# Turning the gated output of the linear attention: TensorE transposes, or 32x32 blocks on VectorE with a way through device memory

## The chip, the cores and the metric

The kernel runs on one core of one Trainium2 chip. The metric is the device time of one execution in microseconds. The inputs and weights are float32; every large product is made from float32r parts (a rounded high part and the difference to it).

## What is computed

Two layers over 256 positions of width 2048. Each layer projects its input once, runs three groups of heads beside each other, multiplies each group's output with a SiLU gate, and projects the concatenation back:

```python
h = x @ w_in
a_q, a_k, a_v, a_z, b_q, b_k, b_v, b_z, b_lr, m_q, m_z = jnp.split(h, cuts, axis=-1)
y_a = chunk_band_attention(heads_a(a_q), heads_a(a_k), heads_a(a_v), rel_table)      # 8 heads of 128
o_b = gla_chunk_recurrence(heads_k(b_q), heads_k(b_k), b_v, heads_k(log_g))          # 4 heads, values of 128
o_b = o_b * lax.rsqrt(jnp.mean(jnp.square(o_b), axis=-1, keepdims=True) + RMS_EPS) * gla_norm_g
y_m = memory_attention(heads_m(m_q), heads_m(mk), heads_m(mv))                       # 4 heads of 128
y = jnp.concatenate([y_a * silu(a_z), y_b * silu(b_z), y_m * silu(m_z)], axis=-1)
x = layer_norm(DEEPNORM_ALPHA * x + y @ w_out, ln_g, ln_b)
```

The change concerns `y_b * silu(b_z)`, the gated output of the linear attention: four heads of 128 columns, a quarter of the 2048 rows of the output projection.

## The kernel before

Weights stream through SBUF in pieces of 128x1024 values (`piece`, L129). For each, SP's queue loads `raw`, ScalarE rounds it to `wh` (L117), VectorE takes the difference `wl` (L118), and TensorE multiplies with both. Each of the three tiles has four buffers. A projection group of 512 columns is made of eight pieces. `ws_half` (L241) makes half a group with the weights stationary, so that its result has the columns on the partitions; `as_group` (L273) makes a whole group with the activations stationary, so that its result has the positions on the partitions.

After each piece both call `tick` (L52). It lets at most one waiting generator run up to its next `yield`, whose value is the number of ticks until it is due again. At most three generators are active once the linear attention is done, the next in `waiting` start when a place comes free. What a generator emits stands in TensorE's and SP's queues exactly there, since these two are written out in program order; the instructions of VectorE, ScalarE and GpSimd are ordered by a scheduler.

The order of a layer's groups from the place of the change on is: `G_BZ` (the gate of the linear attention, L855), then the gates of the two halves of the chunked attention and of the memory attention (`G_AZ0`, `G_AZ1`, `G_MZ`, two `ws_half` each, L862), then the output projection in four groups (L882 on). The heads of the memory attention (`m_head`, L546) run beside the gates: scores, softmax, a turn of the probabilities by `turned`, seven ticks' wait, casts to two parts, two ticks' wait, products with the values.

`turned` (L505) turns a tile in 32x32 blocks: VectorE transposes the blocks in place (L508), GpSimd's queue writes them to device memory as `home` (L510) and fetches them back in four transfers, one for each group of 32 partitions (L512). Both attentions use it for their probabilities.

`gla_gate` (L482) multiplies the linear attention's output `yraw[0]` (tile `yr0`) with the SiLU of `G_BZ`, positions on the partitions. The output projection wants columns on the partitions, so `gla_turned` (L491), a generator put at the head of `waiting`, turns it: for each half `par` of the heads, four TensorE transposes of 128x128 into one PSUM bank (L498), then one ScalarE instruction for the high part, scaled by the norm's gain (L501), and one on VectorE for the low part (L502). The result is `yq[0]`, the first quarter that the output projection reads.

`gb` (L886) are the rows of the layer norm's gain and offset for the next layer. In the first layer they reuse the buffers of `yraw`, the first those of `yr0`, and are loaded by GpSimd's queue (L888, L889). Tiles `gq` and `gk` hold the linear attention's queries and keys, and are free after it.

Of the kernel before, what the change touches and what calls it, by code (L numbers as in the profile page):

```python
# [8 lines left out]
F32 = mybir.dt.float32  # L9
# [3 lines left out]
AF = mybir.ActivationFunctionType  # L13
ALU = mybir.AluOpType
# [4 lines left out]
P = 128  # L19
D = 2048  # L20
T = 256
# [15 lines left out]
def hybrid_trunk_kernel(  # L37
# [7 lines left out]
    pe, dve, act, pool, sp = nc.tensor, nc.vector, nc.scalar, nc.gpsimd, nc.sync  # L45
# [27 lines left out]
    def enter(name, bufs=1, **kw):  # L73
        return ctx.enter_context(tc.tile_pool(name=name, bufs=bufs, **kw))
# [5 lines left out]
    hd = enter("hd", 1)  # L80
# [9 lines left out]
    def nm(s):  # L90
        uid[0] += 1
        return f"{s}_{uid[0]}"
# [4 lines left out]
    def bank():  # L97
        return psa.tile([P, 512], F32, name=nm("bk"), tag="bk")

    def scratch(shape, dtype=F32):  # L100
        return sc.tile(shape, dtype, name=nm("sc"), tag="sc")
# [4 lines left out]
    ident = cst.tile([P, P], F32, name="ident")  # L106
# [3 lines left out]
    def operand():  # L110

        x = opp.tile([P, 4, 2, T], F32R, name=nm("x"), tag="x")
        return x[:, :, 0], x[:, :, 1], x.rearrange("p j h t -> p j (h t)")
# [376 lines left out]

    def gla_turned(yraw, ng, y):  # L491

        for par in range(2):
            on = yraw[:, 2 * par:2 * par + 2].rearrange("p t (b d) -> p t b d", d=P)
            pt = bank()
            for t in range(2):
                for b in range(2):
                    pe.transpose(pt[:, b * T + t * P:b * T + (t + 1) * P], on[:, t, b], ident)  # L498
            ptv = pt.rearrange("p (b t) -> p b t", b=2)
            hi, lo = (x.rearrange("p (b r) t -> p r b t", r=2)[:, par] for x in y[:2])  # L500
            act.activation(hi, ptv, AF.Copy, scale=ng[:, 0:1])  # L501
            dve.scalar_tensor_tensor(lo, ptv, ng[:, 0:1], hi.bitcast(F32), op0=ALU.mult, op1=ALU.subtract)  # L502
            yield 1

    def turned(dst, src, n):  # L505

        blocks = scratch([P, 4, n])
        dve.transpose(blocks.rearrange("p b (g j) -> p g b j", j=32), src.rearrange("p (g b j) -> p g b j", b=4, j=32))  # L508
        home = drm.tile([P, 4, n], F32, name=nm("home"), tag=f"home{n}")
        pool.dma_start(home, blocks)  # L510
        for b in range(4):
            pool.dma_start(dst[b * 32:(b + 1) * 32], home[:, b].rearrange("(a i) n -> i a n", a=4))  # L512
# [107 lines left out]
    def columns(n):  # L620
        return slice(n * 512, (n + 1) * 512)

    def wo_pieces(l, n):

        if n < 3:
            return [w512[l, G_WO + n, pc] for pc in range(8)]
        return [[w256[l, i, pc // 2][:, pc % 2 * 512:pc % 2 * 512 + 512] for i in range(2)] for pc in range(8)]
# [141 lines left out]
    for l in range(L):  # L769
# [20 lines left out]
        gq = hd.tile([P, 2, T], F32, name=nm("gq"), tag="gq")  # L790
        gk = hd.tile([P, 2, T], F32, name=nm("gk"), tag="gk")
# [17 lines left out]
        def heads(g):  # L809
            t = hd.tile([P, 4, T], F32, name=nm("qk"), tag="qk", bufs=4)  # L810
            for i, a, b in ws_group(w512[l, g], xq):
                total(t[:, i:i + 2], a, b)
            return t
# [22 lines left out]
        yraw = [per.tile([P, 4, T], F32, name=nm("yr"), tag=f"yr{i}") for i in range(4)]  # L836
# [3 lines left out]
        for half in range(2):  # L840
            values(2 + half)
            q = heads(G_AQ0 if half == 0 else G_AQ1)
            k = heads(G_AK0 if half == 0 else G_AK1)
# [14 lines left out]
        gla_gate(acc, yraw[0])  # L858
        yq = [operand()]
        gens[0] = [gla_turned(yraw[0], gp[2], yq[0])]  # L860
        waiting[:0] = gens[0]
        for i, g in ((1, G_AZ0), (2, G_AZ1), (3, G_MZ)):  # L862
            y = operand()
# [18 lines left out]
        for n in range(WO_N):  # L882
            if last:
                g, b = scratch([P, 512]), scratch([P, 512])
            else:
                both = per.tile([P, 2, 512], F32, name=nm("gb"), tag=f"yr{n}")  # L886
                g, b = both[:, 0], both[:, 1]
# [3 lines left out]
            src = wo_pieces(l, n)  # L891
# [30 lines left out]
            if last:  # L922
                r = res[:, 1, columns(n)]
# [90 lines left out]
```

## Time and profile before

| | |
|---|---|
| median of 3 runs | 916.83 us (916.73 to 916.91) |
| the profiled execution | 916.47 us |
| its span, first to last instruction | 914.7 us |
| TensorE busy, matmuls | 907.3 us, 5420 |
| VectorE, ScalarE, GpSimd busy | 601.3, 492.2, 87.8 us |
| mean granted TensorE clock | 0.997 |

A line of a group or of the timeline names the engine, the line of the kernel, the operation, the tile written and the tiles read, then the shape and the count. In a group line the busy time in us and the mean duration of one in ns follow, and behind the next bar the idle time before them with what ended it. In a timeline line the start comes first, then the duration, with idle time before it in brackets. PE is TensorE, DVE VectorE, ACT ScalarE, POOL GpSimd, SP the queue of weight loads; `acc` are the projections' PSUM tiles and `bk` the single banks of all else. A line of the waits has the total, the count and the longest wait in us. A line of a window has TensorE's matmuls, its weight loads, VectorE, ScalarE and GpSimd in that order, then the clock, the DMA engines' busy share and GB/s. A line of transfers has the count, the size of one and the median us from issue to landing.

### The profile page before, as it was taken

The numbers are of one execution on the slowest core, as the hardware profiler recorded it, in microseconds if no ns is written. First come the engines' busy times: TensorE is split into PE (matmuls) and PEld (weight loads), VectorE is DVE, ScalarE is ACT, GpSimd is POOL, SyncE is SP. The second block draws the span as 40 slices with busy tenths as digits, with TensorE's granted clock in tenths as the row PEclk, the third lists the DMA queues.
The fourth block names the chain that finished last, engine by engine and source line by source line (L and its number), as shares of the span: only waits on it lengthen the run. The fifth ranks groups of instructions, "written<-read, shape, count | busy, mean of one in ns | idle before, by whom it ended". The sixth has DMA issues, their size and how long they took to land.

```text
span 914.7 us, 14341 instructions
## 1 busy us (share of the span) xinstructions
PE 907.3 (99%) x5420; PEld 797.9 (87%) x5420; DVE 601.3 (66%) x845; ACT 492.2 (54%) x706; POOL 87.8 (10%) x169
## 2 busy tenths in 40 slices
PE   9999999999999999999999999999999999999997
PEld 7889998998888888888888899889888888888885
DVE  6764478656576667555587666885756576766566
ACT  6654475474454666433466445754744455864340
POOL 1000000013031221000000000001121230320000
PEclk9999999999999999999999999999999999999998
DMA  9865865558575778666674466546575766686652
GB/s 302 313 222 168 298 222 165 163 194 251 186 223 182 219 208 251 209 197 193 227 255 166 145 203 202 196 148 212 184 243 190 218 196 198 203 272 202 199 162 92
DMA packets 75989, 189.33 MB, mean 207 GB/s; under 512 B 9224, under 2 KB 33160, under 8 KB 75664
## 3 DMA queue, kind: packets, MB, share of 16 engines
q1 hardware_dynamic: 69120, 173.30, 58.5%
q0 software_dynamic: 6656, 14.86, 5.9%
q8 instruction: 42, 0.69, 0.3%
q10 hardware_dynamic: 144, 0.26, 0.1%
q14 instruction: 27, 0.22, 0.1%
HBM read 181.01 MB, written 7.34 MB: 206 GB/s over the span
## 4 chain that ended last, share of the span: by engine, by line
PE 98%; DMA 1%; SPq 0%; DVE 0%; ACT 0%; issue 0%
PE acc L95 90%; PE bk L95 7%; DMA raw<-w 1%; PE bk L599 0%; PE bk L498 0%; SPq L165 0%; SPq L178 0%; PE bk L397 0%; SPq L180 0%; ACT res L755 0%; ACT wh L117 0%; DVE stats L740 0%; PE bk L344 0%; DVE res L739 0%; DVE res L691 0%
## 5 line engine op out<-in xcount | busy, mean ns | idle before, releaser
L118 DVE TENSOR_TENSOR wl<-raw,wh 128x1024 fp32r<-128x1024 f32 (+3 forms) x321 | 369.5, 1153 | 230.3 <-ACT wh L117 227.4
L117 ACT CAST wh<-raw 128x1024 fp32r<-128x1024 f32 (+3 forms) x321 | 318.9, 995 | 327.9 <-PE acc L95 237.1
L95 PE MATMUL acc<-x,wh 128*128 128x512 f32 x1248 | 396.5, 399 | 0.0
L95 PE MATMUL acc<-wh,x 128*128 128x512 f32 (+2 forms) x1236 | 356.6, 370 | 0.6 <-ACT wh L117 0.6
L95 PEld LDWEIGHTS acc<-x,wl 128*128 128x128 f32 x1248 | 234.4, 188 | 55.2
L95 PEld LDWEIGHTS acc<-wh,x 128*128 128x128 f32 x1236 | 227.2, 188 | 28.4 <-ACT wh L117 1.1
L95 PE MATMUL acc<-x,wl 128*128 128x256 f32 x1248 | 245.7, 278 | 0.0
L95 PE MATMUL acc<-wl,x 128*128 128x512 f32 (+2 forms) x618 | 228.0, 369 | 0.0
L95 PEld LDWEIGHTS acc<-x,wh 128*128 128x128 f32 x1248 | 192.2, 189 | 1.9 <-ACT wh L117 0.2
L95 PEld LDWEIGHTS acc<-wl,x 128*128 128x128 f32 x618 | 116.1, 188 | 14.6 <-DVE wl L118 0.6
L512 POOL DMA_DIRECT2D pT<-home x96 | 52.4, 553 | 56.7 <-DMA home<-sc 24.3
L510 POOL DMA_DIRECT2D home<-sc x24 | 13.4, 560 | 358.4 <-DVE sc L508 352.9
L531 ACT ACTIVATE sc<-sc,mx 128x128 f32<-128x128 f32 (+1 forms) x32 | 14.4, 449 | 18.0 <-DVE mx L529 18.0
L524 DVE SCALAR_TENSOR_TENSOR sc<-bk,bias 128x384 f32<-128x384 f32 x16 | 8.7, 542 | 11.7 <-PE bk L95 11.7
L386 ACT ACTIVATE sc<-sc 128x512 f32<-128x512 f32 x12 | 7.6, 633 | 14.7 <-DVE sc L384 14.6
L508 DVE STREAM_TRANSPOSE sc<-sc 128x384 f32<-128x384 f32 (+1 forms) x24 | 14.9, 619 | 0.6
L118 DVE TENSOR_TENSOR x<-sc,x 128x512 fp32r<-128x512 f32 x20 | 13.5, 685 | 0.7 <-ACT x L117 0.7
L118 DVE TENSOR_TENSOR x<-res,x 128x512 fp32r<-128x512 f32 (+2 forms) x14 | 10.5, 764 | 5.2 <-ACT x L117 5.2
L304 POOL DMA_DIRECT2D gwraw<-gate_w x6 | 3.1, 522 | 106.0 <-PE bk L587 105.1
L95 PE MATMUL bk<-qk,qk 128*128 128x128 f32 (+1 forms) x64 | 13.1, 327 | 0.0
L632 DVE SCALAR_TENSOR_TENSOR res<-res,acc 128x512 f32<-128x512 f32 x15 | 9.7, 684 | 5.1 <-PE acc L95 5.1
L95 PE MATMUL bk<-pT,asv 128*128 128x256 f32 (+1 forms) x64 | 13.0, 326 | 0.0
(207 smaller groups left out, 573.1 us busy)
## 6 DMA issues: line engine op xcount, KB each, us to landing
raw<-w SPq DMA_DIRECT2D x214, 512.0 KB, 4.3
raw<-w SPq DMA_DIRECT2D x64, 388.0 KB, 3.5
raw<-w SPq DMA_DIRECT2D x83, 256.0 KB, 3.6
bias<-relw SPq DMA_DIRECT2D x16, 192.0 KB, 4.3
home<-sc POOLq DMA_DIRECT2D x16, 192.0 KB, 2.7
pT<-home POOLq DMA_DIRECT2D x64, 48.0 KB, 4.0
res<-xT SPq DMA_DIRECT2D x4, 512.0 KB, 5.2
res<-xn SPq DMA_DIRECT2D x1, 2048.0 KB, 8.6
```

The source lines that it names most:

```text
L95: pe.matmul(o, l, r, start=start, stop=stop, skip_group_check=True)
L117: act.copy(hi, src)
L118: dve.tensor_tensor(lo, src, hi.bitcast(F32), op=ALU.subtract)
L304: pool.dma_start(raw[i * 16:i * 16 + 16], gate_w[l])
L386: act.activation(dd, dd, AF.Abs)
L508: dve.transpose(blocks.rearrange("p b (g j) -> p g b j", j=32), src.rearrange("p (g b j) -> p g b j", b=4, j=32))
L510: pool.dma_start(home, blocks)
L512: pool.dma_start(dst[b * 32:(b + 1) * 32], home[:, b].rearrange("(a i) n -> i a n", a=4))
L524: dve.scalar_tensor_tensor(s, pb[:, :384], SCALE, bias[h], op0=ALU.mult, op1=ALU.add)
L531: act.activation(s[:, own[t]], s[:, own[t]], AF.Exp, bias=mx[:, t:t + 1], accum_out=zs[:, t:t + 1])
L632: dve.scalar_tensor_tensor(r, r, ALPHA, acc, op0=ALU.mult, op1=ALU.add)
```

## The change

`gla_turned` uses `turned` instead of TensorE. For each half the gated output (positions on the partitions, two tiles of 2x128 columns) is turned into a tile `yT`, in the buffers of `gq` and `gk`, and the generator asks to wait six ticks after each. Then the high and low parts are taken from `yT` in SBUF, a tile of 128x128 at a time, 8 instructions on ScalarE and 8 on VectorE, because the blocks lie in another order there. The PSUM banks of the transposes are no longer used. Nothing else changes; lines behind L504 move down by two.

```diff
     def gla_turned(yraw, ng, y):
 
+        yT = []
         for par in range(2):
-            on = yraw[:, 2 * par:2 * par + 2].rearrange("p t (b d) -> p t b d", d=P)
-            pt = bank()
+            yT.append(hd.tile([P, 4, P], F32, name=nm("yT"), tag=("gq", "gk")[par]))
+            turned(yT[par], yraw[:, 2 * par:2 * par + 2].rearrange("p t d -> p (t d)"), P)
+            yield 6
+        for par in range(2):
             for t in range(2):
                 for b in range(2):
-                    pe.transpose(pt[:, b * T + t * P:b * T + (t + 1) * P], on[:, t, b], ident)
-            ptv = pt.rearrange("p (b t) -> p b t", b=2)
-            hi, lo = (x.rearrange("p (b r) t -> p r b t", r=2)[:, par] for x in y[:2])
-            act.activation(hi, ptv, AF.Copy, scale=ng[:, 0:1])
-            dve.scalar_tensor_tensor(lo, ptv, ng[:, 0:1], hi.bitcast(F32), op0=ALU.mult, op1=ALU.subtract)
+                    hi, lo = (x.rearrange("p k (t a j) -> p k t a j", t=2, j=32)[:, b * 2 + par, t] for x in y[:2])
+                    src = yT[par].rearrange("p a (t b j) -> p t b a j", t=2, j=32)[:, t, b]
+                    act.activation(hi, src, AF.Copy, scale=ng[:, 0:1])
+                    dve.scalar_tensor_tensor(lo, src, ng[:, 0:1], hi.bitcast(F32), op0=ALU.mult, op1=ALU.subtract)
             yield 1
```

## The prediction

> **What bounds the kernel now.** I read the page's busy times and chain first, then who TensorE waited for, then the timeline of TensorE around the lines that the change touches.
>
> ```profile
> span 914.7 us, 14341 instructions
> PE 907.3 (99%) x5420; PEld 797.9 (87%) x5420; DVE 601.3 (66%) x845; ACT 492.2 (54%) x706; POOL 87.8 (10%) x169
> PE 98%; DMA 1%; SPq 0%; DVE 0%; ACT 0%; issue 0%
> PE bk L95 <- DVE eps L768: 1.1, 1, 1.1
> PE acc L95 <- ACT wh L117: 0.6, 2, 0.3
> ```
>
> The chain that ended last is TensorE for 98% of the span. After its start TensorE waits for other engines for well under 1 us. So time is taken off by taking work from TensorE's queue, and put on only by making TensorE wait. A busy TensorE need not be one at its peak, so I price the removed work from the starts of its neighbours, not from its busy time.
>
> **What the change removes: 16 transposes of 128x128 (L498), four batches of four.** The first batch in layer 0 stands one tick before the scores of the third memory head, the second one tick before those of the fourth. A tick here is 16 matmuls of one `ws_half` piece.
>
> ```profile
> 323.49 0.60 PE L498 MATMUL bk<-ident,yr 128*128 128x128 f32 x4
> 323.84 0.71 PE L95 MATMUL acc<-x,wh 128*128 128x512 f32 x2
> 326.73 0.88 PE L95 MATMUL bk<-mk,mq 128*128 128x256 f32 x6
> 330.24 0.60 PE L498 MATMUL bk<-ident,yr 128*128 128x128 f32 x4
> 333.46 0.88 PE L95 MATMUL bk<-mk,mq 128*128 128x256 f32 x6
> 353.68 0.62 PE L95 MATMUL acc<-x,wh 128*128 128x512 f32 x2
> 356.47 0.88 PE L95 MATMUL bk<-sc,mv 128*128 128x256 f32 x6
> 359.98 0.88 PE L95 MATMUL bk<-sc,mv 128*128 128x256 f32 x6
> 774.17 0.60 PE L498 MATMUL bk<-ident,yr 128*128 128x128 f32 x4
> 777.41 0.88 PE L95 MATMUL bk<-mk,mq 128*128 128x256 f32 x6
> 780.91 0.60 PE L498 MATMUL bk<-ident,yr 128*128 128x128 f32 x4
> 784.14 0.88 PE L95 MATMUL bk<-mk,mq 128*128 128x256 f32 x6
> ```
>
> A bare tick takes 356.47 - 353.68 = 2.79 us. Batch plus tick take 3.24, 3.22, 3.24 and 3.23 us, so the batches cost 0.45 + 0.43 + 0.45 + 0.44 = 1.77 us. The lower bound counts only start to start, 323.84 - 323.49 = 0.35 us, four times 1.4 us; the rest is that the pair of matmuls behind a batch comes apart more slowly. The upper bound is the busy time of the group:
>
> ```profile
> L498 PE MATMUL bk<-ident,yr 128*128 128x128 f32 x16 | 2.4, 272 | 0.0
> ```
>
> I take 1.77, between 1.4 and 2.4, because it is measured between the same neighbours with and without a batch.
>
> The Trainium skill, page "VectorE: DVE Perf Modes", sections "The three transpose paths" and "Rules for kernel authors", gives a TensorE transpose of 128x128 in bf16 as 390 ns and advises TensorE for that shape wherever PSUM may take the result, since VectorE turns only 32x32 blocks. By its figure 16 transposes would be an estimated 6.2 us; the trace disagrees, at 0.11 us each in the queue, and the sum goes by the trace.
>
> **What it adds off TensorE, per layer.** VectorE gets two block transposes of 128x512. The two casts of 128x512 on ScalarE and the two differences on VectorE become eight each of 128x128, from SBUF.
>
> ```profile
> L508 DVE STREAM_TRANSPOSE sc<-sc 128x512 f32<-128x512 f32 x8 | 5.7, 711 | 0.3
> L501 ACT ACTIVATE x<-bk,ng 128x512 fp32r<-128x512 f32 x4 | 2.5, 683 | 0.0
> L502 DVE SCALAR_TENSOR_TENSOR x<-bk,ng,x 128x512 fp32r<-128x512 f32 x4 | 2.8, 744 | 0.0
> L531 ACT ACTIVATE sc<-sc,mx 128x128 f32<-128x128 f32 x16 | 6.4, 402 | 18.0 <-DVE mx L529 18.0
> L118 DVE TENSOR_TENSOR sc<-pT,sc 128x256 fp32r<-128x256 f32 x16 | 6.0, 419 | 3.9 <-ACT sc L117 3.9
> ACT wh L117 <- PE acc L95: 237.1, 165, 3.6
> 293.00:365.00 72.00, 72.00 (x429) 63.48 (x428) 49.18 (x69) 47.95 (x73) 16.61 (x31) 1.00 0.76 229
> ```
>
> VectorE: 2 x 0.71 + 8 x (at most 0.42) - 2 x 0.74 = up to 3.3 us more; ScalarE: 8 x (at most 0.40) - 2 x 0.68 = up to 1.9 us more. In the stage from 293 to 365 us they are busy 49 and 48 of 72 us (fourth and fifth column), so both fit in their idle time. ScalarE also saves one change of tables per layer, because the exponentials of the third and fourth memory heads now follow each other without a SiLU between. What hides this is the lead of the weight pieces: four buffers, and what ScalarE mostly waits for is a matmul that frees one (237.1 us in all, the last row but one), so it writes a piece when TensorE has finished the one four before it: about three ticks, 8 us ahead. If that cover were gone, up to 5 us a layer would be open. I take 0 (below nothing too little to see, since VectorE and ScalarE release no TensorE wait that exists).
>
> GpSimd gets per turn one write of 256 KB (`home`) and four fetches of 64 KB, two turns a layer. That raises a DMA share of 0.76 in the stage by little: the whole GpSimd queue moves 14.86 MB for 5.9% of the 16 engines' span, and the change adds 4 x 0.52 MB to it.
>
> ```profile
> q0 software_dynamic: 6656, 14.86, 5.9%
> home<-sc POOLq DMA_DIRECT2D x8, 256.0 KB, 4.3
> pT<-home POOLq DMA_DIRECT2D x32, 64.0 KB, 5.3
> gb<-ln_g POOLq DMA_DIRECT2D x4, 256.0 KB, 4.9
> gb<-ln_b POOLq DMA_DIRECT2D x4, 256.0 KB, 6.0
> ```
>
> Queues it is moved past: SP's keeps its order. GpSimd's changes: the first turn goes ahead of the loads of the second `gb`; the second turn's write and the loads of the first `gb` now stand between the fourth memory head's write and its fetches. Those `gb` loads wait for the second turn's block transpose, the last reader of `yr0`. Behind them wait that head's fetches, and behind those the turn's own.
>
> **Where this meets TensorE.** Two places have a due time. First, the fourth memory head: its scores come one tick earlier (no second batch in the planner's way), and its products with the values move from 359.98 to 356.47 - 2 x 0.44 + 0.70 (the third head's six, now ahead of it) = 356.3 us. Its fetched probabilities must be cast before that.
>
> ```profile
> 341.66 0.57 POOL L510 DMA_DIRECT2D home<-sc  x1
> 344.81 2.17 POOL L512 DMA_DIRECT2D pT<-home  x4 [2.59 <-ACT sc L117]
> 351.87 0.71 ACT L117 CAST sc<-pT 128x256 fp32r<-128x256 f32 x2
> 353.14 0.75 DVE L118 TENSOR_TENSOR sc<-pT,sc 128x256 fp32r<-128x256 f32 x2
> 366.27 0.63 PE L95 MATMUL acc<-wh,x 128*128 128x512 f32 x2
> 359.99 1.05 ACT L117 CAST wh<-raw 128x1024 fp32r<-128x1024 f32 x1 [0.55 <-ACT yr L580]
> 363.50 1.05 ACT L117 CAST wh<-raw 128x1024 fp32r<-128x1024 f32 x1 [1.15 <-issue]
> ```
>
> The head's write can't go earlier than now, since the third head's fetches are still issued before it. With 4.3 us for the write and 5.3 for the last fetch, issued 3 x 0.55 us after the first, the data are there at 341.7 + 4.3 + 1.6 + 5.3 = 352.9 us, the casts done about 1.1 us later, 354: 2.3 us to spare, where 6.1 us (359.98 - 353.89) are spare now. Second, the turned output `yq[0]` is the first quarter that the output projection reads, at 366.27 - 0.88 = 365.4 us. The second turn's fetches follow the fourth head's by 2.2 us, land near 355, and ScalarE comes to its eight pieces behind the weight piece that now starts at 359.99, at about 360.5 (0.44 + 0.44 earlier than its end at 361.04, and some copies of 0.3 us); eight at 0.40 end at 363.7, VectorE's last difference 0.4 later: some 1.3 us to spare at least. Cost of both: 0.
>
> The Trainium skill, page "DMA: Bandwidth & Descriptors", section on the anatomy of one DMA through GpSimd, fits 2.0 us plus bytes over 436 GB/s: an estimated 2.6 us for the write and 2.2 us for a fetch. The trace's medians here, 4.3 and 5.3 us, are twice that; by the page the spare time would be about 5 us larger and the second rival below gone.
>
> **The sum.** Profiled execution: 916.47 us, of which 914.7 is the span and 1.8 lies around it; the median of the runs is 916.83, 0.36 above it. Taking off 1.77 gives a span of 912.9, a profiled time of 914.7 and a median of 916.83 - 1.77 = **915.1 us**. By the bounds 1.4 and 2.4 it is 915.4 and 914.4.
>
> **The rivals.**
> *Turned output late.* If ScalarE reaches the eight pieces 2 us later than I think, or each takes more than 0.40 us, the output projection starts late: about 1 us a layer, 916 to 917. For it: only 1.3 us to spare, and VectorE works behind ScalarE piece by piece. Against: the projection's first k-tile needs only the first pieces, and ScalarE idles about 1.1 us in every tick.
>
> *Fourth head late, ending slower.* In GpSimd's queue the head's fetches now stand behind one more write and two `gb` loads that move 256 KB each at the same time. If the head's write lands like those (6.0 us) and its last fetch takes the longest landing that this tile shows, 7.0 us,
>
> ```profile
> DMA to landing us min/median/max: 2.2/4.3/7.0
> ```
>
> the data are there at 341.7 + 6.0 + 1.6 + 7.0 = 356.3, cast at 357.4, against 356.3 due: 1.1 us. If the fetches start only once the second `gb` load has landed, issued three places later (343.3) and landing at 349.3, it is 2.7 us. Twice, that is 2.2 to 5.4 us less 1.8: 917.2 to 920.4. It decides from a landing later than 355.2 us (356.3 less 1.1), eats the gain at 0.9 us a layer and is slower by over 0.2% from 1.8. For it: TensorE runs in order, so nothing fills the hole. Against: the write now lands within 3.2 us (344.81 - 341.66), and layer 1 has no `gb` loads at that place.
>
> *The saving is not on the path.* If weights set TensorE's pace, removed work becomes waiting: 916.8. Against it stands the first view: next to no wait for weights. That the transposes stay is excluded, since the changed kernel's TensorE order has none.
>
> **How the numbers follow.** Clean saving 0.68, turned output late 0.08, fourth head late 0.20, not on the path 0.04. 0.2% is 1.83 us, to 915.0 or 918.7, about what a measurement of this kernel can tell from no change. The clean case straddles the lower one: with 1.77 nearer to its lower bound than to its upper, I put 0.6 of it beyond, 0.41 in all. Slower is the fourth head's case less its mild end (0.06), 0.14; the rest, 0.27 + 0.08 + 0.06 + 0.04 = 0.45, is within. The range takes in the clean case's bounds and the late output: 914.4 to 917.0, leaving out the fourth head's case.
>
> **What would show it.** Right: no L498, TensorE 5404 matmuls, third head's scores to fourth head's one tick plus six matmuls apart (3.5 us, where 6.7 now), the two products with values one tick apart with no idle before them, TensorE's waits still under 1 us each, span 912.9. Wrong: an idle of TensorE before `bk<-sc,mv` with the fetch or a cast as releaser (fourth head), an idle before the first matmul of the output projection behind the eight pieces (turned output), or weight waits `wh`, `wl` growing in the stage after the gate (cover gone).

## The result, and the profile after

The changed kernel takes 914.93 us (median of 13 runs), the kernel before 916.66 in the same comparisons. The ratio is 0.9981, with a 95% interval of 0.9974 to 0.9989: 1.7 us faster, clear of noise, and just inside the 0.2% that the prediction drew as its line. One of the 13 runs took 1476.47 us at a granted clock of 0.569, and is left out of the ratio. The profiled execution took 914.58 us, its span 912.8.

The page after, its first lines, and who TensorE waited for:

```profile
span 912.8 us, 14367 instructions
PE 905.3 (99%) x5404; PEld 796.2 (87%) x5404; DVE 605.2 (66%) x861; ACT 489.5 (54%) x714; POOL 99.0 (11%) x189
PE 98%; DMA 0%; DVE 0%; ACT 0%; SPq 0%; issue 0%
```

```profile
PE bk L95 <- DVE eps L770: 1.1, 1, 1.1
PE acc L95 <- ACT wh L117: 0.7, 2, 0.5
```

TensorE has 16 matmuls fewer, the span is shorter by 1.9 us, and the waits are what they were. The added work shows on VectorE (+3.9 us busy) and on GpSimd (+11.2); ScalarE is 2.7 us lower in all: its pieces cost 2.4 us more, but it loads its tables four times less, at 1.28 us each.

The timeline of TensorE in layer 0 after, where the removed batches stood: scores of the third and fourth memory head, their two products with the values, and the first matmuls of the output projection.

```profile
326.18 0.87 PE L95 MATMUL bk<-mk,mq 128*128 128x256 f32 x6
329.68 0.87 PE L95 MATMUL bk<-mk,mq 128*128 128x256 f32 x6
352.68 0.88 PE L95 MATMUL bk<-sc,mv 128*128 128x256 f32 x6
356.19 0.88 PE L95 MATMUL bk<-sc,mv 128*128 128x256 f32 x6
365.27 0.62 PE L95 MATMUL acc<-wh,x 128*128 128x512 f32 x2
```

Scores to scores are 3.50 us, one tick and six matmuls, where 6.73 stood before; no row has an idle time in brackets. The products come at 356.19 and the projection at 365.27, within 0.15 us of the times that the prediction worked out (356.3 and 365.4).

The timelines of GpSimd, ScalarE and VectorE after, around the two due times:

```profile
336.75 2.20 POOL L514 DMA_DIRECT2D pT<-home  x4 [2.44 <-DMA home<-sc]
338.94 1.12 POOL L512 DMA_DIRECT2D home<-sc  x2
340.05 0.54 POOL L890 DMA_DIRECT2D gb<-ln_g  x1
340.58 0.54 POOL L891 DMA_DIRECT2D gb<-ln_b  x1
344.87 2.21 POOL L514 DMA_DIRECT2D pT<-home  x4 [3.74 <-DMA home<-sc]
```

```profile
354.17 0.71 ACT L117 CAST sc<-pT 128x256 fp32r<-128x256 f32 x2 [3.18 <-DMA pT<-home]
361.45 2.44 ACT L503 ACTIVATE x<-yT,ng 128x128 fp32r<-128x128 f32 x8
```

```profile
354.61 0.76 DVE L118 TENSOR_TENSOR sc<-pT,sc 128x256 fp32r<-128x256 f32 x2 [2.35 <-ACT sc L117]
362.81 2.19 DVE L504 SCALAR_TENSOR_TENSOR x<-yT,ng,x 128x128 fp32r<-128x128 f32 x8
```

The fourth head's write and the second turn's are issued together at 338.94, the loads of the first `gb` straight behind them, and the head's fetches only at 344.87, when its write has landed (5.3 us after its issue). ScalarE then waits 3.18 us for the data, casts them at 354.17, and VectorE is done at 355.37, 0.82 us ahead of the products. The last difference of the turned output ends at 365.00, 0.27 us ahead of the projection. Nothing came late, but the cover is thin.

The stage in windows of 4 us (the last two columns are the DMA engines' busy share and GB/s), first after, then before, goes with the slow fetches:

```profile
340.00:344.00 4.00, 4.00 (x25) 3.51 (x24) 3.03 (x4) 3.79 (x6) 1.13 (x3) 1.00 0.91 299
344.00:348.00 4.00, 4.00 (x25) 3.51 (x24) 3.06 (x5) 2.46 (x3) 3.13 (x6) 1.00 0.92 261
348.00:352.00 4.00, 4.00 (x25) 3.47 (x24) 2.20 (x2) 1.23 (x2) 1.26 (x3) 1.00 1.04 286
352.00:356.00 4.00, 4.00 (x27) 3.55 (x26) 1.15 (x4) 1.83 (x4) 1.42 (x3) 1.00 1.05 288
```

```profile
340.00:344.00 4.00, 4.00 (x25) 3.51 (x24) 3.70 (x6) 2.78 (x5) 2.22 (x5) 1.00 0.58 172
344.00:348.00 4.00, 4.00 (x25) 3.47 (x24) 3.36 (x5) 3.33 (x6) 2.17 (x4) 1.00 0.92 317
348.00:352.00 4.00, 4.00 (x25) 3.52 (x24) 1.92 (x3) 2.37 (x4) 1.11 (x2) 1.00 0.95 293
352.00:356.00 4.00, 4.00 (x24) 3.48 (x24) 3.11 (x5) 2.12 (x4) 0.32 (x1) 1.00 0.92 159
```

Before, the share is already 0.92 to 0.95 from 344 to 356 us, which the mean of 0.76 over the stage hid from the prediction. After, the engines are full from 348 to 356 us, and the head's last fetch lands 7.5 us after its issue, where it took 5.2.

### The profile page after: what moved, and what is told of

It is laid out like the page before. It is cut to its first block, busy times and chain, and to the rows that moved or that the text cites. A ratio compares the mean times of both kernels' runs of the same rounds, so it can differ in the third digit from the quotient of the medians.

```text
span 912.8 us, 14367 instructions
## 1 busy us (share of the span) xinstructions
PE 905.3 (99%) x5404; PEld 796.2 (87%) x5404; DVE 605.2 (66%) x861; ACT 489.5 (54%) x714; POOL 99.0 (11%) x189
## 4 chain that ended last, share of the span: by engine, by line
PE 98%; DMA 0%; DVE 0%; ACT 0%; SPq 0%; issue 0%
PE acc L95 90%; PE bk L95 8%; DMA raw<-w 0%; PE bk L601 0%; PE bk L397 0%; SPq L178 0%; ACT res L757 0%; ACT wh L117 0%; DVE stats L742 0%; PE bk L344 0%; DVE res L741 0%; DVE res L693 0%; DVE mvt L696 0%; SPq L165 0%; PE bk L745 0%
## 5 line engine op out<-in xcount | busy, mean ns | idle before, releaser
L512 POOL DMA_DIRECT2D home<-sc x28 | 15.7, 561 | 361.6 <-DVE sc L510 357.9
L118 DVE TENSOR_TENSOR x<-raw,x 128x1024 fp32r<-128x1024 f32 x5 | 6.1, 1212 | 10.5 <-ACT x L117 10.5
```

The source lines that it names most:

```text
L118: dve.tensor_tensor(lo, src, hi.bitcast(F32), op=ALU.subtract)
```

## The experiments

The theory to test: the gain is the TensorE time of the removed batches, 0.44 us each, and nothing that was added lies on the path. The rivals: the gain comes from something else that the edit moved; or the added work does cost, and the gain is a remainder.

**Half the dose.** Layer 0 as changed, layer 1 as before (`gla_turned_pe` is the generator of the kernel before).

```diff
-        gens[0] = [gla_turned(yraw[0], gp[2], yq[0])]
+        gens[0] = [(gla_turned_pe if l else gla_turned)(yraw[0], gp[2], yq[0])]
```

> Layer 0 turns the gated output on VectorE and through device memory, layer 1 keeps the eight TensorE transposes. Theory (each batch of four transposes takes 0.44 us out of TensorE's queue, and nothing that was added shows): two batches gone, 0.88 us, 915.8 us beside 916.7 for the kernel before and 914.9 for the changed one. Rival (the gain comes from one of the layers alone, say from ScalarE's saved change of tables or a shifted transfer in layer 1): the time is at one of the two ends, 914.9 or 916.7.

Measured: 915.36 us beside 916.41, ratio 0.9989 (0.9980 to 0.9998), span 913.4. About 1.0 us, between the ends, as two batches should give. The interval alone does not exclude the full gain (0.9981).

**The transposes back, unread.** The new way stays, and TensorE makes the old transposes beside it.

```diff
         for par in range(2):
+            unread(par)                      # bank(), 4 x pe.transpose, nothing reads it
             yT.append(hd.tile([P, 4, P], F32, name=nm("yT"), tag=("gq", "gk")[par]))
```

> The changed kernel, and beside its new way TensorE still makes the 16 transposes, into banks that nobody reads, the first batch of a layer at its old place, the second four ticks later. Theory (the gain is the removed TensorE work and only that): all of it is back, four batches at 0.44 us, 916.7 us, the time of the kernel before. Rival (the gain comes from the shifted order, fewer changes of tables on ScalarE, or casts that no longer read PSUM): it stays at 914.9.

Measured: 917.00 us beside 916.41, ratio 1.0004 (0.9996 to 1.0013), span 914.8 where the kernel before has 914.7. All of the gain is gone, while ScalarE's saved tables, the casts from SBUF and the new order of the queues are still there. So the gain is the removed TensorE work, and the rest of the edit is worth nothing either way that these runs can tell.

**The added work twice.** Each turn is made two times into the same tile.

```diff
-            turned(yT[par], yraw[:, 2 * par:2 * par + 2].rearrange("p t d -> p (t d)"), P)
+            for _ in range(2):
+                turned(yT[par], yraw[:, 2 * par:2 * par + 2].rearrange("p t d -> p (t d)"), P)
             yield 6
```

> The changed kernel with each turn of the gated output made twice, the second over the first with the same values: the work added off TensorE is doubled (four more block transposes, writes of 256 KB and sets of fetches in all). Theory (this work is hidden, but with little to spare: in layer 0 the fourth head's casts now end 0.8 us before its products, the last piece of the turned output 0.3 us before the output projection begins): one more write ahead of the fourth head's fetches and one more set of fetches behind cost 0.5 to 2 us a layer, 916 to 918 us. Rival (there is more to spare than the trace shows, since only the first piece must be there when the projection begins): 914.9. Rival (the DMA engines are the limit): weight waits grow in the stage, 918 or more.

Measured: 914.97 us, ratio 0.9985 (0.9976 to 0.9994), span 912.8: no cost. My expectation of 0.5 to 2 us a layer failed, the rival with more to spare held. ScalarE's timeline of this run shows the output projection's quarter finished behind its start:

```profile
354.42 0.71 ACT L117 CAST sc<-pT 128x256 fp32r<-128x256 f32 x2 [2.95 <-DMA pT<-home]
361.71 1.27 ACT L504 ACTIVATE x<-yT,ng 128x128 fp32r<-128x128 f32 x4
364.16 0.70 ACT L504 ACTIVATE x<-yT,ng 128x128 fp32r<-128x128 f32 x2 [1.18 <-DMA yT<-home]
365.70 0.69 ACT L504 ACTIVATE x<-yT,ng 128x128 fp32r<-128x128 f32 x2
```

TensorE began the projection at 365.23 and waited for none of this: it needs the first k-tile then, and each further one six matmuls, about 1.4 us, later. So the 0.27 us to spare was the wrong measure for that place. The fourth head's data came only 0.25 us later than with one turn; its fetches still stand ahead of the second turn's.

**The pieces earlier.** The wait of `gla_turned` is four ticks, not six. The line stands in the loop over the two turns, so the edit shortens both waits: the second turn is issued two ticks earlier, the pieces four.

```diff
             turned(yT[par], ...)
-            yield 6
+            yield 4
```

> The changed kernel with the second wait of the turned output's generator four ticks, not six: the high and low parts stand 5.6 us earlier in the planner's order. Theory (nothing waits for them in the changed kernel): 914.9 us, no change; ScalarE may come to them before the fetches have landed and hold weight pieces up, which the lead of 8 us hides. Rival (the pieces, ending 0.3 us before the output projection, hold its first matmuls up by a little): 0.3 to 0.6 us faster.

Measured: 914.92 us, ratio 0.9983 (0.9973 to 0.9992), span 913.1. No change, as the theory has it.

**The heads' due time a tick earlier, after and before.** How near is the fourth head really?

```diff
         turned(pT, s.rearrange("p t m -> p (t m)"), 128)
-        yield 7
+        yield 6
```

> The changed kernel with the memory heads' casts and products due one tick (2.79 us) earlier after their scores. Theory (in layer 0 the fourth head's probabilities are cast at 355.4 us and due at 356.2, so 0.8 us are to spare; in layer 1 2.9): due at 353.4 in layer 0, TensorE idles about 2 us there and about 0 in layer 1, 916.9 us. Rival (more to spare than that, or ScalarE and VectorE take the fetched data earlier when asked earlier): 914.9.

> The kernel before with the same edit. Theory (6.1 us to spare in layer 0 with the transposes on TensorE, 4 in layer 1): no change, 916.7 us. Rival (the fetch was as near its due time before, so the change is not what used the spare time up): 918 or more.

Measured: on the changed kernel 917.97 us (916.30 to 919.21, a wide spread), ratio 1.0015 (1.0006 to 1.0024); on the kernel before 916.30, ratio 0.9997 (0.9987 to 1.0006). So the second rival's mechanism is real and the change brought it within one tick: the same edit costs nothing before and more than the whole gain after. The waits, and TensorE's timeline of the changed kernel with the edit (profiled span 917.3 us):

```profile
PE bk L95 <- ACT sc L117: 1.8, 1, 1.8
PE acc L95 <- ACT wh L117: 1.2, 1, 1.2
```

```profile
353.26 1.23 PE L95 MATMUL bk<-sc,mv 128*128 128x256 f32 x6 [1.77 <-ACT sc L117]
...
355.38 1.05 PE L95 MATMUL acc<-x,wh 128*128 128x512 f32 x2
...
356.66 1.05 PE L95 MATMUL acc<-x,wh 128*128 128x512 f32 x2
...
358.66 0.63 PE L95 MATMUL acc<-x,wh 128*128 128x512 f32 x2
359.36 0.63 PE L95 MATMUL acc<-x,wh 128*128 128x512 f32 x2
```

The wait was expected at 2 us and is 1.77, in layer 0 alone. What was not expected is what follows it: the same pair of matmuls recurs every 1.28 us (356.66 - 355.38) where it takes 0.70 (359.36 - 358.66), for some 4.7 us. From 353.26 to 358.66 the products and four pairs take 5.40 us, where they need 3.5 at the usual pace. So the wait and the slow matmuls behind it make 1.8 + 1.9 = 3.7 of the 4.5 us by which this span is longer than the changed kernel's. The weight wait of 1.2 us stands at the kernel's start (10.73 us), far from the edit, and accounts for 0.7 more: the same pair of matmuls starts at 13.67 us, at 12.97 in the changed kernel's trace. The profiled execution, at 919.13 us, lies at the upper end of the spread; between the medians the edit costs 3.0 us. Why the executions differ so much was not settled.

**The second turn later.** As the changed kernel with the heads a tick earlier, and the second turn issued three ticks later, so that the fourth head's fetches stand straight behind its write.

```diff
-            yield 6
+            yield (9, 3)[par]
```

> As the run with the memory heads' casts and products a tick earlier, and the second turn of the gated output is issued three ticks later (the generator waits nine and three ticks, not six and six), so that in layer 0 the fourth head's fetches are issued straight behind its own write, ahead of the second turn's write and the loads of the first gb. Theory (these three stretch the head's write from about 3 to about 6 us and are what makes the fetch late): the data land some 3 us earlier, the wait of 1.8 us and the slow matmuls behind it are gone, 914.9 us, or a little over if the turned output then comes late. Rival (the head's earlier due time alone makes the wait, the queue does not matter): still 917 to 918.

Measured: 914.74 us, ratio 0.9979 (0.9970 to 0.9988), span 913.5, no wait at the products. The fourth head's rows of GpSimd and of ScalarE in this run:

```profile
336.84 0.57 POOL L512 DMA_DIRECT2D home<-sc  x1
343.37 2.17 POOL L514 DMA_DIRECT2D pT<-home  x4 [5.96 <-ACT sc L117]
349.25 0.71 ACT L117 CAST sc<-pT 128x256 fp32r<-128x256 f32 x2 [2.32 <-DMA pT<-home]
```

and in the run with the heads a tick earlier, without the later turn:

```profile
336.86 1.12 POOL L512 DMA_DIRECT2D home<-sc  x2
343.48 2.19 POOL L514 DMA_DIRECT2D pT<-home  x4 [4.45 <-ACT wh L117]
352.50 0.71 ACT L117 CAST sc<-pT 128x256 fp32r<-128x256 f32 x2 [2.69 <-DMA pT<-home]
```

The cure works, but not as I explained it. The head's write lands 6.0 us after its issue in both and the fetches are issued at the same time, so the write was not sped up by taking three transfers away from behind it. It is the fetches that land sooner, with the second turn's write and fetches and the `gb` loads out of their way: 3.0 to 4.1 us after their issue, where 7.0 to 7.3 without the later turn. The DMA share from 344 to 352 us falls from about 1.0 to 0.74, and ScalarE starts on the data 3.25 us earlier. (The planner also put the products 2.6 us later here, so part of the spare time is that; but VectorE has the data done at 351.03, which would have met the earlier due time, 351.5, too, by 0.5 us.) Why the write takes 6 us in both was not settled.

**The same exchange at a second place.** The first layer's output is turned for the second by 32 TensorE transposes (`transposed`, L583). Two quarters of it, 16 transposes, go over `turned`, issued during the memory values' group.

```diff
     def transposed(xq, gbT):
         raw, gT = gbT
+        yield 4
+        xT = {}
+        for q in (2, 3):
+            xT[q] = hd.tile([P, 2, 512], F32, name=nm("xT"), tag="qk", bufs=4)
+            for t in range(2):
+                with tc.high_priority(AHEAD // 4):
+                    turned(xT[q][:, t].rearrange("p (a n) -> p a n", a=4), res[:, t, columns(q)], P)
+                yield 1
...
-            gens = [transposed(xq, gbT), restored(gb)]           # behind the values' group
-            waiting.append(gens[0])
+            gens = [transposed(xq, gbT), restored(gb)]           # ahead of it
+            waiting.append(gens[0])
```

> The same exchange at a second place: of the 32 TensorE transposes that turn the first layer's output for the second, the 16 of the last two quarters go over VectorE and device memory too, four turns issued during the memory values' group, five to eight ticks ahead of their use. Theory (TensorE's queue is the bound, a batch costs 0.45 us there, and a turn is free where its result is due late enough): four more batches gone, 1.8 us, 913.1 us. Rival (the added transfers, 2 MB within some 25 us at a DMA share of 0.5 to 0.8, delay the weights or the turned quarters come late): 914.9 or more, with waits of TensorE for weights or for the quarters in that stage.

Measured: 912.75 us beside 916.41, ratio 0.9959 (0.9946 to 0.9971), span 910.9: 1.9 us less than the changed kernel's span, for four batches. It is the fastest version here, and the theory's price per batch agrees, within the interval, at a place it was not taken from.

**All four quarters.** As the last, for all four quarters and with no wait ahead.

```diff
     def transposed(xq, gbT):
         raw, gT = gbT
-        yield 4
         xT = {}
-        for q in (2, 3):
+        for q in range(4):
```

> As the run that turns two quarters of the first layer's output off TensorE, now all four: eight turns, no TensorE transposes of it left. Theory (0.45 us a batch while the cover holds): 1.8 us less than with two quarters, 911.0 us. Rival (the cover breaks: 4 MB within some 25 us beside weights at a DMA share of 0.5 to 0.8, and eight block transposes in a row, 5.7 us of VectorE ahead of the next weight pieces, against a lead of 8 us): TensorE waits for weights or for the first quarter by 1 us or more, and each such wait is followed by slow matmuls, so the time is 912.8 or above.

Measured: 925.78 us (924.36 to 928.86), ratio 1.0096 (1.0079 to 1.0112). The cover broke. TensorE's waits, and one window of its stage, in this run:

```profile
PE acc L95 <- DVE x L118: 7.1, 2, 4.0
PE acc L95 <- DVE sc L263: 1.9, 1, 1.9
PE acc L95 <- DVE wl L118: 1.5, 1, 1.5
PE acc L95 <- ACT wh L117: 1.3, 1, 1.3
```

```profile
503.00:510.00 7.00, 5.44 (x27) 4.50 (x26) 3.94 (x7) 2.80 (x4) 4.05 (x9) 0.88 1.03 277
```

The turned quarters (`x`) come 7.1 us late in two waits, VectorE frees a projection's PSUM tile 1.9 us late (`sc L263`), and a weight piece (`wl`) comes 1.5 us late. The 1.3 us behind `wh` stand at the kernel's start, at 10.77 us. In the window the DMA engines are full (share 1.03) and the granted clock is 0.88; with two quarters the same window has a share of 0.60. The four waits of the stage are 10.6 us of the 15.9 by which this span is longer than with two quarters, and the slow matmuls behind three of them an estimated 5.7 us more (by the granted clocks of the last section), against 1.8 saved. How much of the lateness the eight block transposes in a row made, and how much the transfers, was not taken apart.

## Why the prediction was right, point by point

**The term of the sum** was right to the width of the measurement: 1.77 us predicted, 1.73 measured between the medians, 1.9 between the spans. What made it right was to price a batch from the starts of its neighbours (a tick with it less a tick without). The group's busy time, 2.4, would have been a third too high, start to start, 1.4, a fifth too low. The 390 ns a transpose that the Trainium skill's page "VectorE: DVE Perf Modes" ("The three transpose paths") gives for bf16 would have made it an estimated 6.2 us; the runs disagree with that size, for fp32 in a full queue. That the added work is worth nothing was tested on its own by the unread transposes and by the doubled turns.

**The costs at nothing** held, with sizes a little off. ScalarE's eight pieces take 2.44 us, at a pitch of 0.305 (bound: 0.40), VectorE's eight 2.19, at 0.27 (bound: 0.42). ScalarE saves two table loads a layer, not one: four exchanges between exponentials and SiLU became two.

**The turned output's place** was right for ScalarE (it ends at 363.89, predicted 363.7) and not for VectorE, which took a weight piece first and ended at 365.00, not 364.1: 0.27 us ahead of the projection where 1.3 were worked out "at least". It cost nothing because that spare time was beside the point: with the doubled turns ScalarE made its last pieces until 366.39, 1.2 us into the projection, and TensorE did not wait. The prediction's argument against its own rival (only the first pieces are due at first) was the right reading.

**The fourth head's place** is where the steps failed and the errors cancelled. "The head's write can't go earlier than now" was wrong: the third head's write landed after 2.4 us, not 5.1 as before (that no `gb` load was issued just ahead of it is the likely reason, and was not tested alone), so its fetches were issued at 336.75, not 339.47, and the fourth head's write at 338.94, not 341.66. On the other side that write landed after 5.3 us and its fetches were issued 5.9 us behind it, where the prediction had 4.3; the last fetch landed after 7.5 us and not 5.3. These are nearly the values that the rival assumed (6.0 and 7.0); only the earlier start, which the prediction had excluded, kept it from happening. That this place cost nothing was luck as far as the prediction goes. The spare time was 0.82 us, where 2.3 was worked out. One tick less of cover makes the rival true, at 917.97 us, so its chance of 0.2 was not too high.

**The price of that rival** was wrong twice. A wait of TensorE was charged at its length, but the run with the earlier heads shows 1.77 us of idle cost about 3.7 us. And it was charged for both layers, while that run has the wait in layer 0 alone.

**The chances.** The result lies 0.19% below, within the 0.2% by a hair, which the clean case straddled. A forecast this near a line can't say on which side it falls; the side was luck.

## What to carry to other kernels

Where TensorE's queue is full from end to end, moving small transposes off it paid here, within the noise, the time that they took between their neighbours, however long the detour, as long as every turned tile was due later than it arrived. Before doing it again, take the DMA engines' share in windows as short as a landing, not over the stage: doubling the turns was free here, four more at another place paid again, and eight there cost 13 us against the four. The planner's waits are the cheapest thing to move when the cover runs thin: one edit of two numbers gave back all that a tick less had cost, in part by moving the products back.

## What was not expected of the hardware

A short idle of TensorE costs more than itself. Windows of the changed kernel with the heads a tick earlier (TensorE's busy time, the granted clock, the DMA share, GB/s):

```profile
340.00:351.00 11.00, 11.00 (x67) 1.00 1.02 300
351.00:353.30 2.30, 0.53 (x5) 1.00 1.01 289
353.30:358.00 4.70, 4.70 (x19) 0.64 0.89 306
358.00:362.00 4.00, 4.00 (x24) 1.00 0.06 24
```

After 1.77 us without work the granted clock was 0.64 on average over the next 4.7 us, and the pairs of matmuls in it took up to 1.28 us each, 0.70 before and after: by the clock an estimated 1.7 us (4.70 x 0.36) on top of the wait, by the starts of the matmuls the 1.9 above. The run with all four quarters shows the same, and an idle that did not do it:

```profile
475.40:476.93 1.53, 0.00 (x0) 1.00 1.03 388
476.93:482.00 5.07, 5.07 (x29) 1.00 0.79 234
499.16:501.07 1.91, 0.00 (x1) 1.00 1.03 272
501.07:504.50 3.43, 3.43 (x11) 0.53 1.03 299
```

After 1.53 us without work the clock stays at 1.00, after 1.91 it is 0.53. After that run's waits of 3.13 and 4.01 us it is 0.51 and 0.50 over the next 3.4 and 4.9 us; after the 1.21 us at the start of the run with the earlier heads it is 1.00. What sets the border, no run here shows. The Trainium skill, page "TensorE: Matmul & The Clock Gate", part 1 on the clock gate, puts the clock at half after an idle window of about 3.4 us, and back after a busy one of the same length. The halved rate and a return after some 4 us agree with the rows; idles of 1.77 and 1.91 us were enough here.
